# Branch gates with nine of sixteen block pairs by seven products, four of the nine with sums made by transfers

## The chip, the cores and the metric

The kernel runs on one core of one Trainium2 chip. The metric is the device time of one execution in microseconds (us); lower is better. The median of three runs before the change is 2033.77 us.

## The reference

One layer of a hybrid encoder block in float32, 256 tokens by 4096 features. Only what the change touches is spelled out:

```
xn   = rms_norm(x)                                # 256 x 4096
proj = xn @ w_in                                  # 4096 x 14336: q, k, v, z_a, a_c, g_c, z_c, 2048 columns each
y_a  = rms_norm(chunked_attention(q, k, v)) * silu(z_a)
y_c  = rms_norm(conv_module(a_c, g_c))      * silu(z_c)
h    = x + concat(y_a, y_c) @ w_out
out  = rms_norm(h + sigmoid(rms_norm(h) @ w_ple_gate + b) * (p @ w_ple))
```

The change lies in the two branch gates, the columns `z_a` and `z_c` of `proj`: 4096 of its 14336 columns.

## The kernel before

**Products.** A float32 operand is held as a high part and a low part that TensorE takes at its full rate (`x` as `big_t` tiles, a weight tile `wt` as `wh` and `wl`). A product of two blocks is then three matmuls of 128 x 128 by 128 x 512: high by high, low by high, high by low. The high part is a cast on ScalarE (L204), the low part a subtraction on VectorE (L205). Since every weight is used once, this splitting is the main work of both engines.

**Pairs.** `mixed_product` makes 256 x 1024 of a product. Its contraction of 4096 is cut into 16 pairs of two blocks of 128 rows. A pair times two token halves and two column halves is eight block products, 24 matmuls ("plain"). It can also be done as a 2 x 2 by 2 x 2 scheme of seven products, 21 matmuls ("seven"). A seven needs combinations of `x` (`comb_t`, kept in `xS`, made once by `combine_again`) and of the weights. The combinations of the weights are a first pair of sums and a second pair, each split into high and low parts as the weights are (`uh`, `ul`). The seven products are named P1 to P7; P1, P5, P6 and P7 accumulate in four helper banks, P2, P3 and P4 in the banks of three of the four results. P1 uses the high and low parts of the first weight tile, P5 and P7 the first sums, P2 and P3 the second weight tile, P6 and P4 the second sums.

**Two ways to make the first sums.** In an order string `2*` is pair 2 by seven with first sums made by two VectorE additions (L465, L466); `0+` is a pair by seven whose first sums are made by two transfers into `ua`: a plain one on SP's queue (L418) and, when that has landed, an accumulating one on POOL's queue (L419). `sums_ahead` asks for them up to two units early. The second sums are two additions each (L472, L473). Where an order has no `+`, they go to a tile of their own, `ub`. Where it has one, `ub` is `ua`: they are written over the first sums.

**The gates.** `gated` is called four times, each for 1024 columns: twice for `z_a`, twice for `z_c`. Each call is one `mixed_product` over `xT` with the order `dense`, which has eight plain pairs and eight `*` pairs, and no `+`. Two tiles of the tag `u` are there for all the sums. Three `wh`, three `wl`, two `uh` and two `ul` tiles are there for the parts, five `wt` tiles for the weights. The helpers are evicted after the last seven (L1048, L509 to L513), the four results at the end (L1054, L1055), and the four products with `y` (L184) are put off into the next call by `later`, two per unit.

**Order.** Apart from a few pinned places, a planner of the framework orders each engine's instructions when the program is built; every engine then works through its own list in order.

**Room.** The tiles of `xS` lie in `keep` (one) and in the pool `more` of four (three of them). The fourth place of `more` is empty in the gates until `y_ahead` takes it before the last unit of the last call.

Of the kernel before, what the change touches and what calls it, by code (L numbers as in the profile page):

```python
# [17 lines left out]
NB = 512  # L18
# [7 lines left out]
def hybrid_block(  # L26
# [24 lines left out]
    _, T, D = x.shape  # L51
# [16 lines left out]
    def pool(name, bufs, stack=ctx, side=0, **kw):  # L68
        return stack.enter_context(tc.tile_pool(name=name, bufs=bufs, side=sides[side], **kw))
# [14 lines left out]
    more = None  # L84
# [64 lines left out]
    def big_tile(pool=None):  # L149
        return (pool or big).tile([P, 4, 2, T], F32R, tag="big", name="big_t")  # L150
# [29 lines left out]
    later = deque()  # L180
# [77 lines left out]
    def sum_rows():  # L258
        return [spool.tile([P, NB], F32, tag="row", name="comb", bufs=3) for _ in range(2)]

    def combined_parts(dst, at, s, a, a01, a11, g, then=lambda ins: None):

        a00, a10 = a[:, :P], a[:, P:]
        s3, s5, s2, s4 = (s[:, i * P : (i + 1) * P] for i in range(4))
        stt = nc.vector.scalar_tensor_tensor
        then(nc.vector.tensor_tensor(s3, a00, a10, ALU.subtract))
        then(stt(s5, a11, g, a10, ALU.mult, ALU.subtract))
        then(stt(s2, s5, -1.0, a00, ALU.mult, ALU.subtract))  # L270
        then(stt(s4, a01, g, s2, ALU.mult, ALU.add))

        def split():
            hi, lo = dst[:, at : at + 2, 0, :], dst[:, at : at + 2, 1, :]
            src = s.rearrange("q (i t) -> q i t", t=T)
            then(nc.scalar.copy(hi, src))
            then(nc.vector.tensor_tensor(lo, src, hi.bitcast(F32), ALU.subtract))

        return split
# [7 lines left out]
    def combine_again(dst, at, t, i, rows, then=lambda ins: None):  # L287

        a, s = rows
        then(  # L290
            nc.vector.tensor_tensor(
                a.rearrange("q (i t) -> q i t", t=T), t[:, i : i + 2, 0, :].bitcast(F32),
                t[:, i : i + 2, 1, :].bitcast(F32), ALU.add,
            )
        )
        return combined_parts(dst, at, s, a[:, :T], a[:, T : T + P], a[:, T + P :], 1.0, then)

    def comb_tile(combs, n_kept=0):

        if len(combs) < D // NB // 2 - 1 + n_kept:  # L300
            combs.append(big_tile(more))
        else:
            combs.append(keep.tile([P, 4, 2, T], F32R, tag="comb", name="comb_t"))
# [20 lines left out]
    def units(text):  # L324

        return [(int(u.rstrip("*+")), u[-1] if u[-1] in "*+" else "") for u in text.split()]


    dense = units("1 0* 3 2* 5 4* 6* 7 8* 9 10* 11 12* 14* 13 15")
    first = units("0 1 3 5 7 9 11 13 15 2* 8 4* 10 6* 12 14")  # L330
    early = units("1 3 5 0+ 7 9 2+ 11 13 4+ 15 8 6+ 10 12 14")
    early_six = units("1 3 5 0+ 7 2* 9 4+ 11 6* 13 8+ 15 10* 12 14")
# [221 lines left out]
    xT = []  # L554

    xS = {}
# [422 lines left out]
    more = pool("more", 4)  # L979
# [26 lines left out]
    for c0, order in zip(range(0, CW // NB, 2), point):  # L1006
        row = broadcast_row(b_pw, c0 * NB, 2 * NB, tag="stage")
        rows = [row[:, j * NB : (j + 1) * NB] for j in range(2)]
        ys, z = [], []
# [24 lines left out]
    r_c = rstd_of(ssq_c, CW, "r_c")  # L1034


    xS = [xS[0][0]]
    for c in range(2, D // NB):
        if c % 2 == 0:
            comb_tile(xS, 1)  # L1040
        combine_again(xS[c // 2], 2 * (c % 2), xT[c], 0, sum_rows())()

    def gated(ys, c0, col, r_y, order, ahead):

        _, z = sum_tiles()

        def on_helpers(helper):
            nc.scalar.copy(z[0][0], helper["P1"])  # L1048
            helper_sums(helper, z)

        acc = mixed_product(w_in0, col + c0 * NB, xT, xS, order, on_helpers, ahead=ahead, fills=(2,))
        for h, j in QUARTERS:
            zz, y = z[h][j], ys[c0 + j][:, h]
            tt(zz, acc[h][j], zz, ALU.subtract if j else ALU.add)  # L1054
            nc.scalar.activation(zz, zz, AF.Silu, scale=r_x[:, h : h + 1])  # L1055
            if len(y.shape) == 3:
                zz = zz.rearrange("q (g d) -> q g d", d=HD)
            later.append(partial(stt, y, y, r_y[:, h : h + 1], zz, ALU.mult, ALU.mult))

    def before_last(make):  # L1060

        return lambda pair: make(0) if pair == dense[-1][0] else None

    yT, yS = [], []

# [17 lines left out]
    for ys, o_z, r_y in ((y_a, o_za, r_a), (y_c, o_zc, r_c)):  # L1083
        for c0 in range(0, len(ys), 2):
            last = ys is y_c and c0 + 2 == len(ys)
            gated(
                ys, c0, o_z, r_y, dense,
                before_last(y_ahead) if last else None,
            )

# [22 lines left out]
    for c0 in range(0, D // NB, 2):  # L1113
        for j in range(2):
            hc = act.tile([P, NH, NB], F32, tag="act", name="hc")
            c = c0 + j
            nc.sync.dma_start(
                hc, x[0, :, c * NB : (c + 1) * NB].rearrange("(h q) n -> q h n", q=P)
            )
            hs.append(hc)  # L1120

        def on_helpers(helper):
            _, z = sum_tiles()
            h00, h01, h10, h11 = (hs[c0 + j][:, h, :] for h in range(NH) for j in range(2))
            tt(h00, helper["P1"], h00, ALU.add)
            helper_sums(helper, z)
            tt(h01, h01, z[0][1], ALU.subtract)
            tt(h10, h10, z[1][0], ALU.add)
            tt(h11, h11, z[1][1], ALU.subtract)

        acc = mixed_product(
            w_out[0], c0 * NB, yT, yS, dense if c0 else late, on_helpers,
            ahead=y_ahead if c0 == 0 else before_last(h_ahead) if c0 + 2 == D // NB else None,
            fills=(2,),
        )
        for h, j in QUARTERS:
            hc = hs[c0 + j][:, h, :]
            tt(hc, acc[h][j], hc, ALU.add)
            later.append(partial(square_sum, ssq_h[:, h, c0 + j : c0 + j + 1], hc))
# [52 lines left out]
    c0 = n_f - 2  # L1192
# [146 lines left out]
```

## Time and profile before

| | before |
|---|---|
| time, median of 3 (lowest to highest) | 2033.77 us (2033.5 to 2034.0) |
| the profiled execution: time, span | 2032.83 us, 2031.1 us |
| mean granted TensorE clock | 0.998 |
| busy: PE, VectorE (DVE), ScalarE (ACT) | 99%, 92%, 59% |
| matmuls | 9094 |
| DMA issues for sums, `ua`: SP, POOL | 31, 31 (none in the gates) |
| the four calls of `gated` | about 992 to 1323 us of the span |

The page gives the busy time of each engine, the busy tenths in 40 slices, and the chain that ended last. The view by windows gives the same for stretches of the span; the timeline lists instructions with start and duration, several of one kind merged (x2). Idle time before an instruction stands in brackets with what ended it. "DMA to landing" is the time from the issue of a transfer to its arrival.

### The profile page before, as it was taken

Reading aid. Unit: us, or ns where it says so; the run is one execution under the profiler, and the core shown is the slowest. Engines: PE = TensorE matmul, PEld = TensorE weight load, DVE = VectorE, ACT = ScalarE, POOL = GpSimd, SP = SyncE. Lnnn points to the kernel's source line nnn. Section 1 sums busy time; section 2 is a strip of 40 time slices with the busy share of each in tenths; the row PEclk is TensorE's granted clock in tenths of the full one; section 3 lists DMA queues with packets and bytes.
Section 4 is the critical chain, followed back from the end, with each engine's and each line's share of the span. In section 5 each row is a group of like instructions: output and inputs, shape, how many; then the busy total and the mean of one; then the engine's idle time right before and its main releaser. Section 6 shows DMA issues by size and latency. Waiting matters only on the chain.

```text
span 2031.1 us, 26144 instructions
## 1 busy us (share of the span) xinstructions
PE 2015.5 (99%) x9094; PEld 1658.7 (82%) x9094; DVE 1871.1 (92%) x2658; ACT 1203.3 (59%) x1568; POOL 46.0 (2%) x50
## 2 busy tenths in 40 slices
PE   9999999999999999999999999999999999999997
PEld 7888888888888888888888888888888888888876
DVE  7999999679999986868899999999999999999998
ACT  7655555655655445676556566675665666665555
POOL 0000000000000000000000000000000000000000
PEclk9999999999999999999999999999999999999999
DMA  8787878688678867556666666676666656666765
GB/s 294 223 237 233 257 214 251 191 245 239 188 217 250 254 187 207 171 185 205 194 214 198 202 205 214 217 229 209 206 213 201 208 187 207 204 220 205 234 208 179
DMA packets 171167, 436.69 MB, mean 215 GB/s; under 512 B 13966, under 2 KB 17182, under 8 KB 171034
## 3 DMA queue, kind: packets, MB, share of 16 engines
q1 hardware_dynamic: 161952, 417.93, 64.0%
q0 software_dynamic: 8432, 16.25, 4.9%
q8 instruction: 71, 1.16, 0.2%
q10 hardware_dynamic: 650, 0.84, 0.1%
q14 instruction: 62, 0.51, 0.1%
HBM read 430.77 MB, written 4.19 MB: 214 GB/s over the span
## 4 chain that ended last, share of the span: by engine, by line
PE 92%; DVE 5%; issue 2%; ACT 1%; DMA 1%; POOLq 0%; POOL 0%; ACTq 0%; DVEq 0%
PE acc L383 67%; PE acc_P L383 16%; PE acc L229 5%; DVE wl L205 2%; PE tmp_ps L170 1%; DVE cv L721 1%; DMA wt<-in_w_out_dram 0%; PE tmp_ps L890 0%; DVE ul L205 0%; PE tmp_ps L874 0%; PE tmp_ps L908 0%; PE tmp_ps L913 0%; ACT wh L204 0%; PE acc L371 0%; DVE cv L799 0%
## 5 line engine op out<-in xcount | busy, mean ns | idle before, releaser
L383 PE MATMUL acc<-wh,big_t 128*128 128x512 f32 x3992 | 1234.7, 391 | 0.7 <-DVE y_c L1030 0.3
L204 ACT CAST wh<-wt 128x1024 fp32r<-128x1024 f32 (+1 forms) x737 | 713.4, 978 | 550.5 <-PE acc L383 365.0
L205 DVE TENSOR_TENSOR wl<-wt,wh 128x1024 fp32r<-128x1024 f32 (+1 forms) x737 | 821.8, 1127 | 82.0 <-ACT wh L204 78.6
L383 PEld LDWEIGHTS acc<-wh,big_t 128*128 128x128 f32 x3992 | 746.8, 188 | 155.1 <-issue 0.9
L383 PE MATMUL acc<-wl,big_t 128*128 128x512 f32 x1996 | 770.7, 391 | 0.6 <-DVE wl L205 0.5
L383 PEld LDWEIGHTS acc<-wl,big_t 128*128 128x128 f32 x1996 | 374.3, 188 | 79.5 <-DVE wl L205 2.3
L204 ACT CAST uh<-ua 128x1024 fp32r<-128x1024 f32 x160 | 168.3, 1052 | 80.9 <-DVE ua L466 46.1
L721 DVE SCALAR_TENSOR_TENSOR cv<-uT,dw,cv 128x250 f32<-128x250 f32 (+19 forms) x480 | 202.3, 463 | 1.1
L205 DVE TENSOR_TENSOR ul<-ua,uh 128x1024 fp32r<-128x1024 f32 x160 | 194.9, 1218 | 8.4 <-ACT uh L204 8.0
L383 PE MATMUL acc_P<-uh,big_t 128*128 128x512 f32 x516 | 157.9, 391 | 0.0
L204 ACT CAST uh<-ub 128x1024 fp32r<-128x1024 f32 x92 | 96.8, 1053 | 95.8 <-DVE ub L473 86.5
L205 DVE TENSOR_TENSOR ul<-ub,uh 128x1024 fp32r<-128x1024 f32 x92 | 112.2, 1220 | 6.1 <-ACT uh L204 5.2
L383 PEld LDWEIGHTS acc_P<-uh,big_t 128*128 128x128 f32 x516 | 95.8, 188 | 22.3 <-ACT uh L204 3.1
L383 PE MATMUL acc_P<-ul,big_t 128*128 128x512 f32 x258 | 98.8, 391 | 0.1
L229 PE MATMUL acc<-wh,big_t 128*128 128x512 f32 x304 | 93.9, 390 | 0.0
L465 DVE TENSOR_TENSOR ua<-wt 128x512 f32<-128x512 f32 x95 | 65.1, 685 | 18.3 <-DMA wt<-in_w_in_dram 12.4
L383 PE MATMUL acc<-uh,big_t 128*128 128x512 f32 x252 | 78.1, 390 | 0.0
L383 PE MATMUL acc_P<-wh,big_t 128*128 128x512 f32 x252 | 77.8, 389 | 0.0
L229 PEld LDWEIGHTS acc<-wh,big_t 128*128 128x128 f32 x304 | 56.9, 188 | 11.9 <-issue 0.2
L383 PE MATMUL acc_P<-uh,comb_t 128*128 128x512 f32 x216 | 66.4, 390 | 0.1
L466 DVE TENSOR_TENSOR ua<-wt 128x512 f32<-128x512 f32 x95 | 64.9, 683 | 1.1 <-DMA wt<-in_w_in_dram 1.1
L473 DVE TENSOR_TENSOR ub<-ub,wt 128x512 f32<-128x512 f32 x92 | 63.0, 685 | 0.8
(250 smaller groups left out, 1589.3 us busy)
## 6 DMA issues: line engine op xcount, KB each, us to landing
wt<-in_w_in_dram SPq DMA_DIRECT2D x416, 512.0 KB, 4.5
wt<-in_w_out_dram SPq DMA_DIRECT2D x128, 512.0 KB, 4.3
wt<-in_w_ple_gate_dram SPq DMA_DIRECT2D x128, 512.0 KB, 4.2
wt<-in_w_pw_dram SPq DMA_DIRECT2D x32, 512.0 KB, 4.7
ua<-in_w_in_dram SPq DMA_DIRECT2D x31, 512.0 KB, 4.2
ua<-in_w_in_dram POOLq DMA_DIRECT2D x31, 512.0 KB, 8.3
wt<-in_w_in_dram SPq DMA_DIRECT2D x31, 256.0 KB, 2.7
hc<-in_x_dram SPq DMA_DIRECT2D x8, 512.0 KB, 4.8
```

The source lines that it names most:

```text
L170: nc.tensor.transpose(pt[:, i * T + h * P : i * T + (h + 1) * P], src[:, h, b] if len(src.shape) == 4 else src[:, h, b * P : (b + 1) * P], ...
L204: nc.scalar.copy(wh[:, :kc, :], wt[:, :kc, :]),
L205: nc.vector.tensor_tensor(wl[:, :kc, :], wt[:, :kc, :], wh[:, :kc, :].bitcast(F32), ALU.subtract),
L229: nc.tensor.matmul(acc, a, b[:, k, :], start=kb == 0 and kind == 0, stop=kb == kblocks - 1 and kind == 2,)
L383: nc.tensor.matmul(banks[name], a, b, start=name not in begun, stop=final and ends[name] == n and kind == 2 and not (left and name in "P2 ...
L465: plus(ua[:, 0], w0[:, 0], w0[:, 1])
L466: plus(ua[:, 1], w0[:, 1], w1[:, 1])
L473: plus(ub[:, 1], ub[:, 0], w1[:, 0])
L721: nc.vector.scalar_tensor_tensor(cv[:, i, PAD - k :], uT[:, i, : T + k - PAD], dw[:, b, k : k + 1], cv[:, i, PAD - k :], ALU.mult, ALU.add,)
```

## The change

The gates get an order of their own, `gates`, with seven plain pairs, five `*` pairs and four `+` pairs. Pair 1 is the ninth seven; the combination of `x` that it needs is put in the fourth place of `more` and made through `later` in the first units of the first call. `xS` becomes a dictionary by pair.

```
-    dense = units("1 0* 3 2* 5 4* 6* 7 8* 9 10* 11 12* 14* 13 15")         (kept for other products)
+    gates = units("3 0+ 5 2* 4* 7 6+ 8* 9 10+ 1* 11 12+ 14* 13 15")
...
-    xS = [xS[0][0]]
+    tiles = [xS[0][0]]
     for c in range(2, D // NB):
         if c % 2 == 0:
-            comb_tile(xS, 1)
-        combine_again(xS[c // 2], 2 * (c % 2), xT[c], 0, sum_rows())()
+            comb_tile(tiles, 1)
+        combine_again(tiles[c // 2], 2 * (c % 2), xT[c], 0, sum_rows())()
+    xS = {2 * c: (tiles[c // 2], 2 * (c % 2)) for c in range(D // NB)}
+    xS[1] = big_tile(more), 0
+    rest = []
+    later.append(lambda: rest.append(combine_again(*xS[1], xT[0], 2, sum_rows())))
+    later.append(lambda: rest.pop()())
...
-        return lambda pair: make(0) if pair == dense[-1][0] else None
+        return lambda pair: make(0) if pair == 15 else None
...
-                ys, c0, o_z, r_y, dense,
+                ys, c0, o_z, r_y, gates,
```

By instructions, the changed program has 12 matmuls fewer (8997 for 9009 as the program counts them), two VectorE instructions fewer, nine ScalarE casts more and 16 DMA issues more on each of SP and POOL. Before the last pw product and after the first w_out product the lists of all engines are unchanged.

In the second to fourth call the planner's lists now read, from pair 2 to pair 1 (a, b: first and second weight tile; s, t: first and second sums; "acc 7a" are the plain matmuls of a tile):

```
VectorE: ... sums 2s x2, low 2b, low 2s, low 4a, sum 2t, low 4b, sum 2t, low 7a, low 2t, low 7b, sums 4s x2, low 6a,
         low 4s, sums 4t x2, low 4t, low 6s, low 6b, sum 6t, low 8a, sum 6t, low 8b, low 6t, low 9a, sums 8s x2, low 9b,
         low 10a, low 8s, sums 8t x2, low 8t, low 10s, low 10b, sum 10t, low 1a, sum 10t, low 1b, low 10t, low 11a, ...
ScalarE: ... cast 2a, 2b, 2s, 4a, 4b, 7a, 2t, 7b, 6a, 4s, 4t, 6s, 6b, 8a, 8b, 6t, 9a, 9b, 10a, 8s, 8t, 10s, 10b, 1a, 1b, 10t, ...
TensorE: ... P1 2, P5 2, P7 2, P2 2, P3 2, P1 4, P2 4, P3 4, then P6 and P4 of 2 among acc 7a, P5 and P7 of 4 among acc 7b,
         P1 6, then P6 and P4 of 4 around the first two matmuls of P5 6, the rest of acc 7 (12 matmuls),
         P5 6, P7 6, P2 6, P3 6, P1 8, P6 and P4 of 6 among P2 8, P3 8, acc 9a, P5 and P7 of 8 among acc 9b, P1 10,
         P6 and P4 of 8 around the first two matmuls of P5 10, the rest of acc 9, P5 10, ...
```

In the program before, TensorE's list in the gates is the plain order: unit by unit, P1, P5, P7, P2, P3, P6, P4.

## The prediction

> **What bounds the kernel now.** I read the page first (busy time, slices, chain), then the windows of the four calls of `gated`, then who waited for whom there, then the timeline of one call.
>
> ```profile
> span 2031.1 us, 26144 instructions
> PE 2015.5 (99%) x9094; PEld 1658.7 (82%) x9094; DVE 1871.1 (92%) x2658; ACT 1203.3 (59%) x1568; POOL 46.0 (2%) x50
> ...
> PE 92%; DVE 5%; issue 2%; ACT 1%; DMA 1%; POOLq 0%; POOL 0%; ACTq 0%; DVEq 0%
> ...
> 992.00:1073.00 81.00, 80.76 (x356) 66.23 (x355) 74.11 (x89) 48.26 (x55) 0.69 (x1) 1.00 0.63 202
> 1073.00:1155.00 82.00, 82.00 (x362) 67.73 (x362) 78.33 (x94) 49.38 (x55) 0.00 (x0) 1.00 0.64 206
> 200.00:280.00 80.00, 80.00 (x362) 66.40 (x361) 80.00 (x135) 40.73 (x47) 4.87 (x4) 1.00 0.81 236
> ...
> PE acc L383 <- DVE z L1054: 0.2, 1, 0.2
> ...
> PEld acc L383 <- issue: 0.9, 2, 0.6
> PEld acc L383 <- DVE wl L205: 0.4, 1, 0.4
> ```
>
> The chain is TensorE (92%). In the second call, 362 matmuls fill 82.00 us: one per 0.2265 us. The last three rows are all that TensorE and its weight loads waited in the four calls: 0.2 + 0.9 + 0.4 us of 331. So a matmul less there is 0.2265 us less, as long as TensorE's inputs stay on time. That "as long as" is the question: VectorE is busy 78.33 of the 82.00 us. The third window has a product with four `+` pairs beside the convolution: there VectorE is full and TensorE still doesn't wait.
>
> **TensorE's gain.** Per call one pair goes from 24 matmuls to 21: 3 x 4 calls x 0.2265 = 2.72 us less, on the path.
>
> **VectorE's sum.** Durations overlap in part, so what counts is start to start:
>
> ```profile
> 1165.65 0.68 DVE L465 TENSOR_TENSOR ua<-wt 128x512 f32<-128x512 f32 x1
> 1166.26 0.68 DVE L466 TENSOR_TENSOR ua<-wt 128x512 f32<-128x512 f32 x1
> 1166.86 0.68 DVE L472 TENSOR_TENSOR ub<-ua,wt 128x512 f32<-128x512 f32 x1
> 1167.57 0.69 DVE L473 TENSOR_TENSOR ub<-ub,wt 128x512 f32<-128x512 f32 x1
> 1168.18 1.22 DVE L205 TENSOR_TENSOR ul<-ua,uh 128x1024 fp32r<-128x1024 f32 x1
> 1169.32 1.22 DVE L205 TENSOR_TENSOR wl<-wt,wh 128x1024 fp32r<-128x1024 f32 x1
> 1170.45 1.22 DVE L205 TENSOR_TENSOR ul<-ub,uh 128x1024 fp32r<-128x1024 f32 x1
> ...
> 1166.97 1.05 ACT L204 CAST uh<-ua 128x1024 fp32r<-128x1024 f32 x1 [2.85 <-DVE ua L466]
> 1167.92 1.05 ACT L204 CAST wh<-wt 128x1024 fp32r<-128x1024 f32 x1
> ```
>
> Narrow ones (512) follow each other in 0.605 us (1165.65 to 1166.86 for two), wide ones (1024) in 1.135. A plain pair is two wide: 2.27. A `*` is three wide and five narrow: 6.43. A `+` has two narrow fewer: 5.22. Eviction and the products with `y` are twelve narrow ones, about 7.3 a call. Before: 8 x 2.27 + 8 x 6.43 + 7.3 = 76.9 us a call. After: 7 x 2.27 + 5 x 6.43 + 4 x 5.22 + 7.3 = 76.2, against 357 matmuls x 0.2265 = 80.9 us of TensorE. Summed over a call VectorE still fits, with 4.7 us to spare. The new combination of `x` comes once, in the first call, where no products with `y` are left from a call before (four narrow ones less): its cost is covered by those.
>
> ```profile
> L277 DVE TENSOR_TENSOR big_t<-comb,big_t 128x512 fp32r<-128x512 f32 x20 | 13.5, 686 | 1.6 <-ACT big_t L276 1.6
> L291 DVE TENSOR_TENSOR comb<-big_t 128x512 f32<-128x512 f32 x15 | 10.3, 685 | 0.1
> L268 DVE TENSOR_TENSOR comb<-comb 128x128 f32<-128x128 f32 x30 | 8.5, 285 | 0.9 <-ACT comb L284 0.7
> ```
>
> That is two of 0.69 and four small ones near 0.28, 2.5 us at most. Without the cover it would take half of the first call's spare 4.7.
>
> **What the sum hides: the order within a call.** With a `+` in the order, every `*` writes its second sums over its first ones. So the second sums can't be begun until the first ones are split; before, all four additions ran in a row, as the rows at 1165.65 to 1167.57 show, and the splits came later. The step times of this chain:
>
> ```profile
> 1219.96 0.62 PE L383 MATMUL acc<-uh,big_t 128*128 128x512 f32 x2
> ...
> 1220.61 1.06 ACT L204 CAST uh<-ub 128x1024 fp32r<-128x1024 f32 x1 [0.30 <-PE acc L383]
> ...
> 1221.70 1.23 DVE L205 TENSOR_TENSOR ul<-ub,uh 128x1024 fp32r<-128x1024 f32 x1
> ```
>
> TensorE's last reading start to ScalarE's cast: the two matmuls end at 1220.58, the cast starts 0.03 later; one matmul lasts 0.39, so 0.42. Cast to VectorE: 1220.61 to 1221.70, 1.09. An addition that needs the one before it: 1166.86 to 1167.57, 0.71 instead of 0.605. An addition to the cast behind it: 1166.26 to 1166.97, 0.71.
>
> *Pairs 2 and 4 follow each other.* The first weight tile of pair 7 takes the `wh` that P3 of pair 2 releases. From the start of that P3's last matmul: release 0.42, cast 1.09, three wide (low 7a, low 2t, low 7b) 3.41, one addition 0.61, the next one to its cast 0.71 and to the subtraction 1.09, the subtraction and its end 1.25, two dependent additions 0.71 + 0.71, the cast of pair 4's second sums 1.06 and 0.05 to TensorE. Together 11.1 us. TensorE has 43 matmuls from there to P6 of pair 4 in its new order: 9.74 us. It comes 1.4 us too early and waits.
>
> *Then three groups of plain, `+`, `*`* (7 6 8; 9 10 1; 11 12 14). Eight wide and eight narrow ones: 9.08 + 4.84 = 13.92. In the list nothing stands between the last addition of a `*` and the low part of its second sums, which needs the cast: 0.71 + 1.09 in place of 0.61, 1.2 us idle. The two dependent additions give 0.1 each. That is 15.3 us a group; TensorE has 66 matmuls, 14.95. With no lead left after pair 4, each group costs the difference, 0.4 us, and it is TensorE that waits (P6 of pairs 8, 1 and near 14). A group later the plain pairs 13, 15 and 3 let VectorE catch up, but TensorE's loss stays.
>
> The Trainium skill, page "VectorE: DVE Perf Modes", section "The DRAIN you can't avoid", says that a semaphore between chained Vector instructions costs nothing extra, since each waits for the pipe to empty anyway. The rows above differ: 0.71 for the dependent pair against 0.605. By the page the groups would lose 0.2 less each, 2.4 us less in all; I keep the rows.
>
> A wait costs more than itself:
>
> ```profile
> 1033.37 0.61 PE L383 MATMUL acc<-wh,big_t 128*128 128x512 f32 x2
> 1034.01 0.50 PE L383 MATMUL acc<-wl,big_t 128*128 128x512 f32 x1
> 1034.35 0.62 PE L383 MATMUL acc<-wh,big_t 128*128 128x512 f32 x2
> ```
>
> After this short wait the next matmul follows after 0.34, 0.11 more than usual.
>
> *Sum.* Pair 4: 1.4 in three calls; in the first call the list has other low parts between pair 4's sums, and I take 0.5 between none and 1.4. Together 4.7. Groups: 12 x 0.4 = 4.8. Restarts: 15 x 0.11 = 1.7. Less 2.72. Net +8.5 us. On the profiled execution, 2032.83 (1.7 outside its span of 2031.1), that is 2041.3; the median of the runs is 0.9 above that execution: 2042.2.
>
> *Bounds.* Below: none of it reaches TensorE, as in the window with four `+`: 2031.05. A gain beyond the matmuls is limited to the 1.5 us of waits that exist. Above: the subtraction of the chain late by as much again as a cast slot (0.4 us for pair 4 and 0.3 for each group, from casts that queue behind one another 0.95 apart, rows 1166.97 and 1167.92): 3 x 1.8 + 1 + 12 x 0.7 + 1.7 - 2.7 = 13.8, or 2047.6.
>
> **The transferred sums.** Each `+` adds one issue on SP and one on POOL.
>
> ```profile
> L418 SPq DMA_DIRECT2D ua<-in_w_in_dram x31: 367/368/379, 83.5 to 795.9; - x31
> ...
> DMA to landing us min/median/max: 3.7/4.2/5.9
> ...
> L419 POOL DMA_DIRECT2D ua<-in_w_in_dram x31: 1213/1222/1359, 88.6 to 800.4; - x31
> ...
> DMA to landing us min/median/max: 6.1/8.3/9.9
> ```
>
> From SP's issue to the finished sum: 4.2 + 8.3 = 12.5 us, between 9.8 and 15.8. The sum of pair 10 may be issued when pair 4's second sums are split (its place is theirs) and is cast right behind pair 8's second sums: one group less one subtraction, 15.3 - 1.3 = 14.0 us. That holds in the middle and fails by up to 1.8 at the end. Pair 12 is the same behind pair 8; pairs 0 and 6 have longer. Queued behind a late sum: on ScalarE the casts of 10b, 1a, 1b; on VectorE low 10s and all behind; on SP pair 10's own weights, which need places that come free only later. POOL's queue holds only these and one small power, which the third call needs. SP itself is busy 0.37 us with each issue, and the weights lie in five places as before.
>
> The Trainium skill, page "DMA: Bandwidth & Descriptors", section "Anatomy of one DMA — SWDGE (gpsimd) path", fits 2.0 us plus bytes over 436e3 for a transfer from this queue; for 0.5 MB that would be an estimated 3.2 us. The row has 8.3, with accumulation; by the page lateness would be excluded, by the row it isn't.
>
> **Rivals.** *The cover holds (0.33).* VectorE has 4.7 us to spare a call, and the window with four `+` shows no wait. Then the gain is whole or nearly: 2031.1, not slower than before. It decides where the waits of a call stay under 0.68 us, the three matmuls. For it: the sum and that window. Against: in that window each `+` stands between plain pairs and convolution fills VectorE's idle places; here `2* 4*` and `10+ 1*` touch.
>
> *Transferred sums come late (0.07).* Two a call, eight in all; if each is late as at the maximum, 1.8 us, that adds 14 to the forecast: 2056; if a third are late by 1 us, 2.7: 2045. For it: a lead of 14.0 against 12.5 to 15.8. Against: the median fits.
>
> *The change doesn't do what it says:* excluded, the program has 12 matmuls fewer.
>
> **Numbers.** Forecast (VectorE's chain late): 0.60, 2042.2, in itself 2036 to 2047.6. Cover holds 0.33, late sums 0.07. The range 2031 to 2047.6 takes in both main cases and leaves out the late sums and the ends. A measurement can tell about 0.2%, 4.1 us: faster by that needs more than the 2.72 and most of the old waits, 0.04; within, the cover's case less that and the forecast's lowest edge, 0.36; slower, 0.60.
>
> **What would show it.** Right: in the after trace TensorE waits for `uh` or `ul` at P6 of pairs 4, 8 and 1 in calls two to four, about 3 us a call; VectorE's idle time before L205 `ul` is put down to ScalarE's cast; calls of about 83 to 84 us. Wrong: calls of 81 us with no such waits; or casts of `ua` put down to a DMA, which would be the late sums. Outside the gates nothing should move.

## The result, and the profile after

| | before | changed |
|---|---|---|
| median (lowest to highest of six) | 2033.73 us (2032.80 to 2034.34) | 2045.06 us (2044.22 to 2045.89) |
| ratio | | 1.0056, 95% interval 1.0046 to 1.0067 |
| profiled execution: time, span | 2032.83, 2031.1 us | 2044.22, 2042.4 us |

The change makes the kernel 11.3 us slower. The page of the changed kernel, its head and the shares of the chain:

```profile
span 2042.4 us, 26162 instructions
PE 2021.8 (99%) x9082; PEld 1651.7 (81%) x9082; DVE 1873.3 (92%) x2656; ACT 1208.5 (59%) x1577; POOL 66.0 (3%) x66
...
PE 88%; DVE 7%; issue 2%; DMA 1%; ACT 1%; POOLq 0%; ACTq 0%; POOL 0%; DVEq 0%; SPq 0%
```

There are 12 matmuls fewer, and VectorE's busy time is what it was (1871.1 before). But TensorE's share of the chain fell from 92% to 88% and VectorE's rose from 5% to 7%: the loss is waiting, not work. The next view is the one by windows, each window one call of `gated`, from the first matmul of its first result bank to that of the next call. Columns: length, busy time of PE, weight loads, VectorE, ScalarE, POOL with their instructions, granted clock, DMA share, GB/s.

```profile
990.59:1072.82 82.23, 82.23 (x359) 66.31 (x357) 76.33 (x90) 49.16 (x59) 5.96 (x5) 1.00 0.79 237
1072.82:1156.70 83.88, 82.91 (x359) 65.75 (x357) 77.98 (x91) 49.79 (x56) 4.88 (x4) 1.00 0.78 235
1156.70:1241.43 84.73, 83.32 (x358) 65.74 (x357) 78.27 (x91) 50.16 (x56) 4.87 (x4) 1.00 0.79 237
1241.43:1329.24 87.81, 86.44 (x386) 68.42 (x384) 81.66 (x105) 56.19 (x71) 3.66 (x3) 1.00 0.76 232
```

Cut in the same way, the calls before:

```profile
989.87:1072.82 82.95, 82.38 (x362) 67.26 (x360) 76.06 (x92) 49.62 (x60) 0.69 (x1) 1.00 0.63 201
1072.82:1154.56 81.74, 81.74 (x361) 67.51 (x361) 78.07 (x93) 49.12 (x55) 0.00 (x0) 1.00 0.65 206
1154.56:1236.28 81.72, 81.72 (x362) 67.59 (x361) 78.34 (x93) 49.19 (x55) 0.00 (x0) 1.00 0.64 207
1236.28:1319.67 83.39, 83.39 (x378) 69.27 (x378) 78.92 (x101) 51.65 (x64) 0.00 (x0) 1.00 0.66 218
```

So the first call gained 0.7 and the others lost 2.1, 3.0 and 4.4: 8.9 us of the 11.3. Where the end of one call and the beginning of the next are interleaved, another cut would move up to 0.9 us from one to the other. The first of the four w_out products, right behind the gates, is as long as before (90.57 for 90.52). Of the rest, 0.7 lies ahead of the gates, where the program is the same, and 1.5 in the third and fourth w_out products, where weight tiles came late in this execution. Who waited for whom in the four calls (total us, times, longest):

```profile
DVE ul L205 <- ACT uh L204: 16.6, 16, 1.2
...
PEld acc_P L384 <- ACT uh L204: 14.4, 41, 1.2
...
ACT uh L204 <- DMA ua<-in_w_in_dram: 6.1, 4, 2.4
PEld acc_P L384 <- DVE ul L205: 3.3, 15, 0.4
PE acc_P L384 <- ACT uh L204: 2.7, 5, 0.7
```

Before, TensorE and its weight loads had 1.5 us of waits of any kind in the gates. Now VectorE stands idle 16 times, four times a call, about 1 us each, until ScalarE has cast a sum, and TensorE and its weight loads wait behind it for `uh` and `ul`. A weight load that waits need not delay a matmul, so these rows aren't yet the loss. Taken from start to start, TensorE's matmuls of the four calls lost 10.9 us against one per 0.2265 us, for 1.8 before: about 5 in waits for `uh`, 4.0 in stops of 0.05 to 0.14 us, the rest in smaller ones. The timeline at P6 of pair 4 in the second call (start, duration; idle time before it and its releaser in brackets) shows the chain:

```profile
1098.91 1.23 DVE L205 TENSOR_TENSOR ul<-ua,uh 128x1024 fp32r<-128x1024 f32 x1 [0.52 <-ACT uh L204]
...
1100.17 0.69 DVE L473 TENSOR_TENSOR ua<-ua,wt 128x512 f32<-128x512 f32 x1
...
1100.90 0.69 DVE L474 TENSOR_TENSOR ua<-ua,wt 128x512 f32<-128x512 f32 x1
...
1101.69 0.40 PE L384 MATMUL acc_P<-wl,big_t 128*128 128x512 f32 x1
1101.70 2.00 ACT L204 CAST uh<-ua 128x1024 fp32r<-128x1024 f32 x2 [2.82 <-DVE ua L474]
1102.78 1.23 DVE L205 TENSOR_TENSOR ul<-ua,uh 128x1024 fp32r<-128x1024 f32 x1 [1.19 <-ACT uh L204]
...
1102.80 0.50 PE L384 MATMUL acc_P<-uh,big_t 128*128 128x512 f32 x1 [0.71 <-ACT uh L204]
```

Low part of the first sums, then the two second sums over them, then the cast, then both VectorE and TensorE go on. TensorE's starts are 1.11 us apart (1101.69 to 1102.80) where 0.227 is usual.

### The profile page after: what moved, and what is told of

It reads as the page before. It is cut to its first block, busy times and chain, and to the rows that moved or that the text cites. A ratio compares the mean times of both kernels' runs of the same rounds, so it can differ in the third digit from the quotient of the medians.

```text
span 2042.4 us, 26162 instructions
## 1 busy us (share of the span) xinstructions
PE 2021.8 (99%) x9082; PEld 1651.7 (81%) x9082; DVE 1873.3 (92%) x2656; ACT 1208.5 (59%) x1577; POOL 66.0 (3%) x66
## 4 chain that ended last, share of the span: by engine, by line
PE 88%; DVE 7%; issue 2%; DMA 1%; ACT 1%; POOLq 0%; ACTq 0%; POOL 0%; DVEq 0%; SPq 0%
PE acc L384 64%; PE acc_P L384 15%; PE acc L229 5%; DVE wl L205 2%; PE tmp_ps L170 1%; DVE cv L722 1%; DVE ul L205 1%; DMA ua<-in_w_in_dram 1%; ACT uh L204 1%; DMA wt<-in_w_in_dram 0%; DVE ua L474 0%; PE tmp_ps L891 0%; DVE ua L473 0%; ACT wh L204 0%; DVE ua L467 0%
## 5 line engine op out<-in xcount | busy, mean ns | idle before, releaser
L384 PEld LDWEIGHTS acc<-wh,big_t 128*128 128x128 f32 x3944 | 738.1, 188 | 154.5 <-DVE z L1060 1.7
L384 PE MATMUL acc<-wl,big_t 128*128 128x512 f32 x1972 | 759.7, 391 | 0.9 <-DVE wl L205 0.9
L204 ACT CAST uh<-ua 128x1024 fp32r<-128x1024 f32 x200 | 209.0, 1051 | 136.9 <-DVE ua L474 88.2
L205 DVE TENSOR_TENSOR ul<-ua,uh 128x1024 fp32r<-128x1024 f32 x200 | 244.1, 1225 | 25.6 <-ACT uh L204 24.8
L204 ACT CAST uh<-ub 128x1024 fp32r<-128x1024 f32 x60 | 63.1, 1052 | 56.1 <-DVE ub L474 47.4
L420 POOL DMA_DIRECT2D ua<-in_w_in_dram x47 | 57.4, 1222 | 869.9 <-DMA ua<-in_w_in_dram 360.2
L384 PE MATMUL acc<-uh,big_t 128*128 128x512 f32 x260 | 81.1, 391 | 0.0
L205 DVE TENSOR_TENSOR ul<-ub,uh 128x1024 fp32r<-128x1024 f32 x60 | 73.3, 1222 | 5.2 <-ACT uh L204 4.6
L229 PEld LDWEIGHTS acc<-wh,big_t 128*128 128x128 f32 x304 | 56.9, 188 | 11.8 <-issue 0.2
L466 DVE TENSOR_TENSOR ua<-wt 128x512 f32<-128x512 f32 x83 | 57.1, 688 | 6.9 <-DMA wt<-in_w_out_dram 4.9
L384 PEld LDWEIGHTS acc_P<-ul,big_t 128*128 128x128 f32 x270 | 50.2, 188 | 14.4 <-DVE ul L205 4.1
```

The costliest lines, as they stand in the source:

```text
L204: nc.scalar.copy(wh[:, :kc, :], wt[:, :kc, :]),
L205: nc.vector.tensor_tensor(wl[:, :kc, :], wt[:, :kc, :], wh[:, :kc, :].bitcast(F32), ALU.subtract),
L229: nc.tensor.matmul(acc, a, b[:, k, :], start=kb == 0 and kind == 0, stop=kb == kblocks - 1 and kind == 2,)
L384: nc.tensor.matmul(banks[name], a, b, start=name not in begun, stop=final and ends[name] == n and kind == 2 and not (left and name in "P2 ...
L420: nc.gpsimd.dma_start(ua, columns(col, step + apart), accum_op=ALU.add)
L466: plus(ua[:, 0], w0[:, 0], w0[:, 1])
```

## The experiments

All are timed against the kernel before; the ratio is to the runs of it that were taken along with each kernel, so it isn't the quotient of the medians shown. A call is cut as above; "next" is the first w_out product, behind the four calls, "five" the sum of all. Two sevens touch when no plain pair stands between them. Three theories of the loss are tested: A, the second sums written over the first ones make VectorE's chain late; B, the transferred first sums are late; C, nine sevens are too much work for VectorE.

| kernel | median us | ratio, 95% interval | calls 1 to 4 | next | five |
|---|---|---|---|---|---|
| before | 2033.73 | 1 | 82.95, 81.74, 81.72, 83.39 | 90.52 | 420.3 |
| changed | 2045.06 | 1.0056 (1.0046 to 1.0067) | 82.23, 83.88, 84.73, 87.81 | 90.57 | 429.2 |
| e1 second sums in a tile of their own | 2044.13 | 1.0049 (1.0035 to 1.0062) | 90.50, 82.37, 82.51, 83.99 | 90.09 | 429.5 |
| e2 transferred sums in one place of their own | 2112.46 | 1.0383 (1.0369 to 1.0398) | 109.43, 99.68, 99.69, 100.93 | | |
| e3 before, second sums in place | 2040.42 | 1.0027 (1.0015 to 1.0038) | 83.33, 83.43, 83.69, 86.24 | 90.33 | 427.0 |
| e4 all nine `*` | 2037.23 | 1.0014 (1.0006 to 1.0023) | 81.39, 82.55, 82.48, 84.80 | 91.69 | 422.9 |
| e5 as e1, other room | 2036.72 | 1.0015 (1.0006 to 1.0023) | 81.76, 83.15, 82.87, 85.64 | 88.39 | 421.8 |
| e6 as e5, two `+` | 2039.64 | 1.0032 (1.0019 to 1.0044) | 81.88, 83.52, 83.72, 87.46 | 88.43 | 425.0 |
| e7 last call as before | 2039.96 | 1.0034 (1.0021 to 1.0046) | 82.21, 84.86, 85.19, 84.77 | 89.98 | 427.0 |
| e8 no `*` touches a `*` | 2075.58 | 1.0210 (1.0196 to 1.0224) | 83.15, 90.20, 95.97, 95.88 | | |
| e9 as e4, three touches | 2042.00 | 1.0043 (1.0029 to 1.0056) | 83.47, 82.18, 81.50, 90.00 | 90.65 | 427.8 |
| e10 three touches, two `+`, own tile | 2033.35 | 0.9999 (0.9990 to 1.0008) | 81.52, 81.12, 81.10, 85.01 | 89.48 | 418.2 |
| e11 as e10, last call as before | 2034.13 | 1.0003 (0.9994 to 1.0012) | 81.77, 81.60, 82.32, 85.69 | 88.98 | 420.4 |
| e12 as e10, in place | 2063.38 | 1.0148 (1.0134 to 1.0161) | 83.61, 88.95, 89.20, 92.25 | | |

**e1: second sums in a tile of their own.**

```
+    first_more.close()                        # the pool of four ...
+    more = pool("more", 3)                    # ... opened anew with three
...
+    room = ExitStack()
+    gx = pool("gx", 1, room)                  # in the place of the fourth tile of `more`
+    xS[1] = gx.tile([P, 2, 2, T], ...), 0
...
-            if seven == "*" and not sums:
+            if seven == "*" and own is not None:
+                ub = own.tile([P, 2, NB], F32, tag="u", name="ub")
```

> The changed kernel, with one thing undone: in the gates the second sums of a `*` pair go to a tile of their own (4 KB beside the ninth combination, which now takes 4 KB instead of a place of 8 KB), not over the first sums. Second sums of the `+` pairs stay in place. Theory A (second sums written over the first ones make VectorE's chain late): the waits of about 1.0 us a call before P6 of pair 4 and 0.4 us each before P6 of pairs 8 and 1 go, calls two and three take 81 to 82 us instead of 83.9 and 84.7, and the time is 2033 to 2037 us. Theory B (first sums that come by transfer are late): the places of `u` come free somewhat sooner, so up to the 1.1 us of the third call that was put down to a transfer; 2043 to 2045 us. Theory C (VectorE has too much work with nine sevens, in whatever order): no change, 2044 to 2046 us.

The median hardly moved, which by itself speaks for theories B and C. The windows of its calls tell another story:

```profile
990.20:1080.70 90.50, 85.74 (x358) 66.85 (x357) 85.88 (x120) 54.10 (x66) 18.69 (x5) 0.98 0.75 221
1080.70:1163.07 82.37, 82.37 (x359) 66.30 (x357) 77.72 (x91) 50.47 (x56) 4.88 (x4) 1.00 0.81 243
1163.07:1245.58 82.51, 82.25 (x358) 66.38 (x357) 77.66 (x91) 50.34 (x56) 4.87 (x4) 1.00 0.80 242
1245.58:1329.57 83.99, 83.99 (x375) 68.06 (x373) 80.80 (x103) 53.68 (x66) 3.66 (x3) 1.00 0.78 241
```

Calls two to four are 7.5 us shorter than in the changed kernel (248.9 for 256.4), as theory A has it (its 81 to 82 us for calls two and three are missed by 0.4 to 0.5), with the same amount of VectorE work (77.7 us busy). The first call is 8.3 longer, with 120 VectorE instructions for 90: to make the room I had closed the pool and opened it anew, and the combinations of `x`, which otherwise hide beside the last pw product, had to wait for it and fell into the first call. My edit gave back what it gained.

**e2: transferred sums in a place of their own** (the same room; `ua = sums[m] = (own or upool).tile(...)` for the `+` pairs, second sums in place).

> The changed kernel, with the first sums of the `+` pairs in a place of their own, so that their transfers need not wait for a `*` pair to be done with a `u` tile; second sums stay over the first ones everywhere. Theory A (in-place second sums): the waits before P6 of pairs 4, 8 and 1 stay, only the 6.1 us of ScalarE waits for transfers go, of which TensorE saw about 1 us; 2043 to 2046 us. Theory B (late transfers): the transfers start earlier, most of the loss goes, 2033 to 2037 us. Theory C (too much VectorE work): no change, 2044 to 2046 us.

None of the three. One place is fewer than two: a transfer may start only when the `+` pair before is wholly done. ScalarE waited 83.8 us for transfers (10 times, up to 10.3), and each call lost 17 us and more. The first call also bears e1's room. So e2 doesn't test theory B on the changed kernel; it shows what late transferred sums cost.

**e3: the kernel before with in-place second sums.**

```
-            if seven == "*" and not sums:
+            if seven == "*" and not (sums or inplace):
```

> The kernel before, with one thing of the change alone: in the gates the second sums are written over the first ones. Order, pairs and transfers are those of before (eight `*`, no `+`). Theory A: the pairs 4 and 6, which touch in that order, show the same wait, 1.0 to 1.4 us a call before P6 of pair 6, and 0.11 us for each restart; the others (one plain pair and one `*`: 2.27 + 6.43 + 1.3 of idle = 10.0 us against 45 matmuls, 10.2 us) hold. Four calls: 4.4 to 6 us slower than before, 2038 to 2040 us. Theories B and C: no change, 2033 to 2035 us, since there are no transferred sums and VectorE's sum is the same.

It came out as theory A had it, at the upper end: 5.5 us slower by the ratio (3.1 to 7.7), 6.7 by the medians shown, without a transfer and without a ninth seven. The waits in its four calls:

```profile
DVE ul L205 <- ACT uh L204: 10.2, 11, 1.2
PEld acc_P L383 <- ACT uh L204: 7.5, 16, 1.5
...
PEld acc_P L383 <- DVE ul L205: 3.6, 11, 0.5
...
PE acc_P L383 <- ACT uh L204: 2.1, 2, 1.1
```

VectorE's idle time before `ul` is there again, as in the changed kernel. But the wait at pair 6 was 1.26 and 1.15 us in calls one and four and small in the two between; smaller ones stand at other pairs.

**e4: nine `*`.** `gates = units("3 0* 5 2* 4* 7 6* 8* 9 10* 1* 11 12* 14* 13 15")`, so no transfers and second sums in a tile of their own.

> The changed kernel with the same order of the pairs, but all nine sevens are `*`: no transferred sums, and so second sums in a tile of their own, as before the change. VectorE has 7 x 2.27 + 9 x 6.43 + 7.3 = 81.1 us a call against 80.9 us of TensorE. Theory A: no waits of the kind before P6 with a cast between; VectorE is just full, so small waits of a few tenths each, 0.2 to 1.5 us a call: 2031.7 to 2037 us. Theory B: no late transfers, the same. Theory C (VectorE's work): worse than the changed kernel, which has 4.9 us less of it a call: 2047 to 2055 us.

With 4.9 us more VectorE work a call than the changed kernel it is 7.8 us faster (2037.23 for 2045.06, at the upper edge of theory A's range). Theory C, that nine sevens are too much work, falls. Yet calls two and three take 82.5 us for 357 matmuls (80.9): something is left.

**e5: the tile of e1 with its room elsewhere.** The three rows for sums in the late pool (`row`, 6 KB, idle in most of the gates) become one tile, and `ub` is its first 4 KB; all else as in the changed kernel. In e5 and e6 rows of bias and gain of the last product are overwritten before their last use, so that part computes with other values; the work is the same. In e10 and e11 those rows are loaded later, at pair 8.

```
+    kept_rows.append(spool.tile([P, 3, NB], F32, tag="rows", name="rows", bufs=1))
...
-        acc = mixed_product(..., ahead=ahead, fills=(2,))
+        acc = mixed_product(..., ahead=ahead, fills=(2,), own=kept_rows[0][:, :2])
```

> As e1 (second sums of the `*` pairs in the gates in a tile of their own), but the room comes from the three rows for sums of the late pool, kept as one tile, and the places of the combinations of x stay as in the changed kernel. In e1 the first call took 90.5 us, 8.3 more than in the changed kernel, because the combinations of x had to wait for the place that was freed at once; calls two to four took 82.4, 82.5 and 84.0 us instead of 83.9, 84.7 and 87.8. Theory A (in-place second sums): the first call takes 82 to 83 us, the others as in e1: 2034 to 2037 us. Theory A' (the first call pays for the ninth seven in any case): 2042 to 2045 us.

Theory A: the first call is short again (81.76), and 8.3 of the 11.3 us are gone (2045.06 to 2036.72). The waits in its four calls (the cast stands in line 209 here, the subtraction in 210, the matmul in 391):

```profile
PEld acc_P L391 <- DVE ul L210: 5.8, 15, 1.2
ACT uh L209 <- DMA ua<-in_w_in_dram: 5.3, 2, 3.2
...
PEld acc_P L391 <- ACT uh L209: 2.7, 10, 0.3
DVE ul L210 <- ACT uh L209: 2.4, 2, 1.8
```

VectorE's wait for the cast went from 16.6 us to 2.4. Transferred sums are still late twice, and what TensorE waits for now is mostly the low part.

**e6: two transferred sums instead of four.** As e5 with `"3 0* 5 2* 4* 7 6+ 8* 9 10+ 1* 11 12* 14* 13 15"`.

> As e5, with two transferred sums a call instead of four (pairs 6 and 10; pairs 0 and 12 are `*`). VectorE has 2.4 us more work a call, 78.6 us against 80.9 of TensorE. If what is left over the 81 us a call in e1 (1.4 us) comes of VectorE's amount of work: 2037 to 2042 us, slower than e5. If it comes of the transfers or of the order in which the second sums of the `+` pairs are made: 2031 to 2035 us, faster than e5. If of neither (waits of a hundredth to a tenth at every change of operands): the same as e5 within 1.5 us.

2.9 us slower than e5, in the range of "VectorE's amount". e10 shows that the amount alone isn't it: it has the same amount. In calls two and three of e6 TensorE's longer waits stand at pair 8, which touches pair 6: 1.4 and 1.6 us for the low parts of its sums.

**e7: the last call in the old order** (`dense if last else gates`).

> The changed kernel, with the old order (eight `*`, own tiles, no transfers) in the last of the four calls; calls one to three as changed. The fourth call lost 4.4 us against before and the third 3.0. If the 1.4 us beyond the third call's loss come from the end of the gates (the results and the transposes of the first y block meet a late VectorE): the fourth call takes 83.4 to 84 us, and the time is 2045.1 less 4 to 4.4 us = 2040 to 2041.5 us. If the ninth combination's place in the late pool, which the first y block also asks for, made it: the same. If the loss of a call is set by the order of all calls and only shifts: 2043 to 2045 us.

5.1 us of the 11.3 go with the last call, somewhat more than the 4 to 4.4 expected. In the profiled execution the call is 3.0 us shorter than in the changed kernel and the product behind it 0.6. Calls two and three of this profile are 1.0 and 0.5 us longer than in the changed kernel with the same program: so much does the sum of small waits differ from one execution to the next.

**e8: no two `*` touch** (`"3 0+ 5 2* 7 4* 6+ 9 8* 10+ 11 1* 12+ 13 14* 15"`, in place).

> The changed kernel with another order of the same nine sevens, second sums in place: 3 0+ 5 2* 7 4* 6+ 9 8* 10+ 11 1* 12+ 13 14* 15. No two `*` touch and no `*` follows a `+` at once, so that no first sums are made on VectorE while the second sums of the pair before are still to be made there. Theory A with the price of touching pairs: the waits of 1.0 us before P6 of pair 4 and of 0.4 before P6 of 8 and 1 go, three calls of 1.9 us: 2038 to 2041 us; the seven that now stands before the last plain pair may cost some of that at the end of a call. If it is the in-place chain within each pair and not the touching, the waits move to other pairs: 2043 to 2047 us.

Much slower, and neither branch said so. TensorE waits 2 to 4 us at the start of calls two to four, where pair 0's first sums come late by transfer and ScalarE, in order, holds the cast of pair 0's first weight tile behind theirs. e12 shows the same place. These stops are about a quarter of what TensorE lost in the four calls (40 us, start to start). Weight tiles were late as well: ScalarE waited 14.2 us for them, ten times, up to 3.5. So e8 doesn't tell the touching from the in-place chain.

**e9: one touch less.** As e4 in the order `"3 0* 5 2* 7 4* 6* 9 8* 11 10* 1* 13 12* 14* 15"`: one plain pair fewer at the end, so that 2 4 and 6 8 become 2, 4 6 and 8.

> As e4 (all nine sevens `*`, second sums in a tile of their own, no transfers), with another order of the same pairs: 3 0* 5 2* 7 4* 6* 9 8* 11 10* 1* 13 12* 14* 15. Sevens touch at three places of a call instead of four, and one plain pair instead of two stands behind the last seven. In e4 calls two and three took 82.5 us, 1.6 more than 357 matmuls, although the second sums were not in place. If the touching makes what is left (two sevens in a row are 42 matmuls, 9.5 us, for 12.9 us of VectorE's work): 82.0 to 82.3 us a call, 2033 to 2036 us. If VectorE's amount of work does (81.1 of 80.9 us): as e4, 2036 to 2039 us. If the end of a call lacks its second plain pair: slower than e4.

In the middle of the gates as the touching has it (82.18 and 81.50 us for 82.5), but the third branch came true as well: with one plain pair behind the last seven and VectorE just full, TensorE waited at the end of the first call 1.6 us for the results' eviction, and the fourth call took 90.0 us.

**e10: the order of e9, two transferred sums, second sums in a tile of their own** (`"3 0+ 5 2* 7 4* 6* 9 8+ 11 10* 1* 13 12* 14* 15"`).

> The order of e9 with pairs 0 and 8 by transferred sums (VectorE 78.6 us a call), and the second sums of the `*` pairs in the three rows as in e5. The rows of bias and gain of the last product are loaded at pair 8 instead of at its first seven. The place for pair 8's first sums is free when it is asked for, two units ahead. If both VectorE's amount and the touching count: 81.2 to 82 us a call, 2030 to 2034 us, less than e5 and e9. If the single tile for second sums or the touching alone decides: as e9 or 1 to 2 us above.

```profile
990.33:1071.85 81.52, 81.52 (x359) 66.77 (x357) 77.89 (x94) 51.55 (x60) 3.52 (x3) 1.00 0.74 226
1071.85:1152.97 81.12, 81.12 (x359) 66.90 (x357) 79.62 (x95) 50.53 (x56) 2.44 (x2) 1.00 0.72 226
1152.97:1234.07 81.10, 81.10 (x358) 66.91 (x357) 79.64 (x95) 50.59 (x56) 2.44 (x2) 1.00 0.73 228
1234.07:1319.08 85.01, 84.07 (x382) 69.20 (x380) 83.44 (x109) 55.07 (x68) 1.22 (x1) 1.00 0.70 220
```

Calls two and three are as long as their matmuls, 0.6 us shorter than before the change, with VectorE busy 79.6 of 81.1 us: fuller than in the changed kernel, which waited. So it is the chain and the order, not the amount. (The end of the fourth call still has one wait of 1.0 us, for the results' eviction.) It is 11.7 us faster than the changed kernel. Against the kernel before it is the same: its five products are 2.1 us shorter in the trace, and 1.3 of that is given back where a weight tile of the fourth w_out product is late. That spot took between nothing (e2, e3, e11) and 1.3 us over the kernel before in the traces of this study; whether it is chance stays open. Another 0.6 goes between 1620 and 1750 us, behind the w_out products; e5, e6 and e11, with the same room, lose 0.6 to 0.8 there.

**e11: e10 with the last call as before.**

> As e10 in calls one to three, with the old order of eight `*` pairs in the last call (second sums in the three rows). e7 showed that the old order in the last call saves 5.1 us of the changed kernel's 11.3. If the seam to the next product still costs in e10: 0.5 to 2 us below e10. If e10 has no loss at the seam: 0.7 us above e10, for the three matmuls.

0.8 us above e10, where 0.7 was expected without a loss at the seam, the passage to the next product. The two intervals overlap, so this agrees with that branch but doesn't show it.

**e12: e10 in place.** Its order and pairs, `ub` over `ua` and the rows of the last product as in the changed kernel.

> The order and the two transferred pairs of e10, with the second sums over the first ones as in the changed kernel. e10 has the second sums of the `*` pairs in a tile of their own and takes 81.1 us in calls two and three, without a wait. If the in-place sums are a cause by themselves: waits of 0.5 to 1.3 us before P6 of the second pair of each touching two (6, 1 and 14), 2 to 4 us a call, 2040 to 2050 us. If only the touching at four places and the two transfers more made the changed kernel slow: 2033 to 2035 us, as e10.

30 us slower than e10, beyond the range. The waits in its four calls:

```profile
ACT uh L204 <- DMA ua<-in_w_in_dram: 13.7, 3, 4.9
PEld acc_P L384 <- ACT wh L204: 12.7, 3, 5.0
PE acc_P L384 <- ACT wh L204: 11.4, 3, 4.6
PEld acc_P L384 <- ACT uh L204: 10.1, 25, 1.2
DVE ul L205 <- ACT uh L204: 7.7, 7, 1.2
```

In-place sums cost twice here. They make the chain (7.7 us of VectorE before `ul`), and they hold the places of `u` longer: pairs 12 and 14, which touch, each keep one until the low part of their second sums is made. So pair 0's first transfer is issued only 10.1 us before the third call begins (at 1153.9; in e10 17.5 before, at 1135.5), ScalarE waits up to 4.9 us for its sums at the start of the next call, and TensorE stands 11.4 us in three pieces. In e10 ScalarE has no such wait for a transfer and VectorE none before `ul`. The second cost is the larger one: of the 29.5 us that TensorE lost in the four calls, start to start, 11.9 are these three stops, 5.4 the halved clock behind them (last section), and 3.1 are waits for `uh`.

## Why the prediction was right

Forecast 2042.2 us, measured 2045.06, by the mechanism that it named; the terms of its sum fared differently. The range, 2031 to 2047.6, took in both main cases, so a time inside it says little; what speaks for the mechanism are the waits and e3 and e5.

**What bounds the kernel; TensorE's gain.** Right: 357 matmuls a call, 0.2265 us each; e10 shows 81.1 us for them. The gain of 0.68 a call is there in the changed kernel's first call (0.7) and in e10.

**VectorE's sum over a call fits.** Right, and so no measure of the time: e4 and e10 do more of it and are faster.

**The order within a call: in-place second sums.** Right, shown from both sides: putting them in place costs the kernel before 5.5 us (e3), taking them out gives the changed kernel 8.3 back (e5). The idle 1.2 us before `ul` was predicted for three groups a call. In calls two to four it was there for the second sums of pairs 8 and 1 (1.17 us each) and at pair 4, for the first sums (0.52) and for the second ones (1.19), but not at pair 14.

**Pair 4: 1.4 us, mis-sized.** It was 0.88 us in each of calls two to four (starts 1.11 apart less 0.227) and 0.11 for the restart: 2.7 us without restarts, for 4.7 forecast (0.5 of it in the first call).

**Three groups of 0.4: mis-sized.** Worked out start to start, P6 of pairs 8 and 1 waited 0.2 to 0.3 each in calls two to four, and 0.11 for the restart; near pair 14 there was 0.11 at most. That is about 2.4 us with restarts, where nine times 0.5 was forecast. For the third group the step was wrong, not only its size: the prediction has nothing between the last addition and the low part behind it, but at pair 14 a low part of a plain pair stands there and covers the cast (second call):

```profile
1146.62 0.69 DVE L474 TENSOR_TENSOR ua<-ua,wt 128x512 f32<-128x512 f32 x1
1147.22 1.22 DVE L205 TENSOR_TENSOR wl<-wt,wh 128x1024 fp32r<-128x1024 f32 x1
1148.49 1.23 DVE L205 TENSOR_TENSOR ul<-ua,uh 128x1024 fp32r<-128x1024 f32 x1
```

The first call, for which 0.5 and three groups were set, had restarts of about 0.11 only and gained. So the waits at P6 of pairs 4, 8 and 1 with their restarts came to 1.8 us a call, not to the 3 that the prediction named as its sign.

**What made up for it, not foreseen.** Transferred sums were late four times: those of pair 0 at the starts of calls two to four, those of pair 6 in the third. In the third call TensorE lost 0.6 us before P6 of pair 0 and 0.45 before P5 of pair 6: the rival of late sums, priced at 14 us for all eight and at 2.7 for a third of them, was there in small. It was at pairs 0 and 6, to which the prediction gave the longer leads, and not at 10 and 12. That its second price gave 2045 us, the measured time, is chance: TensorE lost 1.05 us to late sums, restarts included. ScalarE's timeline has the casts that waited for a transfer (the third is pair 6's):

```profile
1072.59 1.05 ACT L204 CAST uh<-ua 128x1024 fp32r<-128x1024 f32 x1 [1.46 <-DMA ua<-in_w_in_dram]
...
1157.45 1.06 ACT L204 CAST uh<-ua 128x1024 fp32r<-128x1024 f32 x1 [2.44 <-DMA ua<-in_w_in_dram]
...
1187.53 1.05 ACT L204 CAST uh<-ua 128x1024 fp32r<-128x1024 f32 x1 [0.32 <-DMA ua<-in_w_in_dram]
...
1241.60 1.05 ACT L204 CAST uh<-ua 128x1024 fp32r<-128x1024 f32 x1 [1.87 <-DMA ua<-in_w_in_dram]
```

The fourth call lost 1.4 us more than the third. Most of that is where the cut falls: 28 transposes of the first y block stand ahead of it now, 16 before, 12 more at 0.11 us each. The product behind took as long as before with 14 matmuls fewer (408 for 422), so the time was lost at the seam. Stops of 0.05 to 0.14 us stand at many other P5 and P6 too: in all they are 4.0 us in the four calls (0.5 before), where 1.7 was forecast for restarts. And 2.5 us of the 11.4 between the two profiled executions lie outside the gates, where nothing should have moved. The sum of the gates, 8.9 for 8.5, is right partly because these errors cancel, which is luck.

**The rule on chained instructions.** The Trainium skill, page "VectorE: DVE Perf Modes", section "The DRAIN you can't avoid", would have the second of the dependent additions follow as any other. Here it follows after 0.73 (1100.17 to 1100.90), with 0.605 for independent ones: the row was the one to use.

**The rivals.** The cover doesn't hold. The late sums were priced by the medians of a kernel with long leads; e2 and e12 show that they can become the main cost, tens of us, where a place for them comes free later; e8 is slow in part by them. The chance of 0.07 was for this order only.

**What stays open.** e5 to e10 is 3.3 us, e6 to e10 6.3, for an order with one touching place fewer (it takes a plain pair from the end) and for other transferred pairs, 0 and 8. Only e9 against e4 changes the order alone: its middle calls agree with the touching, and so does the place of e6's waits. Why e6 is slower than e5 isn't shown.

## What to carry to other kernels

Writing a second result over a first one saves a tile but ties three engines into one chain, and it holds the place that the next transfer needs; look for both before the busy sums. An engine with spare time in the sum can be late in every stretch: compare the work between two touching heavy units with the time in which it must be done. When an experiment moves nothing, read its stages before the verdict: e1's own room had hidden the 8 us that its edit gained.

## What the runs showed of the hardware

After a long wait TensorE ran at a granted clock of half for some microseconds. In e12, around the start of the third call (length of window first, granted clock third from the end):

```profile
1165.00:1169.00 4.00, 0.29 (x2) 0.00 (x0) 2.90 (x4) 1.53 (x3) 0.00 (x0) 0.85 0.76 220
1169.70:1174.40 4.70, 4.70 (x13) 3.65 (x12) 1.94 (x3) 2.23 (x3) 0.00 (x0) 0.50 0.38 112
1176.00:1180.00 4.00, 4.00 (x20) 3.30 (x19) 3.87 (x6) 2.48 (x3) 0.00 (x0) 1.00 0.00 0
```

The matmuls were 0.43 us apart instead of 0.227. TensorE had stood 3.8 us. In e1's first call a wait of 1.76 us, with shorter ones just before, was enough:

```profile
1007.10:1010.20 3.10, 3.10 (x8) 2.49 (x9) 3.08 (x8) 1.57 (x2) 2.17 (x1) 0.53 0.65 185
```

In e3 a single wait of 1.1 us left the clock at 1.00, and so did one of 1.6 us in e9. The half clock can begin later than the wait ends: in e12's second call a wait of 3.0 us ended at 1080.9, and the clock was 0.88 from 1081.3 to 1082.8 and 0.50 from 1082.8 to 1085.8. The Trainium skill, page "TensorE: Matmul & The Clock Gate", section "What's actually happening", puts the fall to half rate after about one idle window of 3.4 us that runs free of the kernel; the 3.8 us wait agrees, the 1.76 us one is shorter than that. In e12 the matmuls behind the three waits of 3.0, 3.8 and 4.6 us lost 1.4 to 2.6 us each time beyond the wait itself; behind the 1.1 us in e3 it was only the 0.11 of the restart.
